# Memory values in two steps, pooling products in the logits' banks, and first values behind 24 key products

## The chip, the cores and the metric

The kernel runs on one core of a Trainium2 chip. Its time is device microseconds of one execution. The core has a matrix engine (TensorE, "PE" in the profile, with its weight loads as "PEld"), a vector engine (DVE), a scalar engine (ACT), a general engine (POOL) and a queue that issues transfers (SP). PE writes its products to PSUM, which the profile names by tile tags; DVE and ACT read them from there.

## What is computed

Two layers over 1024 tokens of width 1024. Both have gated cross-attention of four heads (128 wide) into 256 memory tokens. Layer 0 adds a gated causal pooling branch, layer 1 forgetting attention with 16 heads over keys and values that are projected once.

```python
def mixer_sublayer(x, mem, w_in, w_mem_kv, w_out, main_fn):
    h = x @ w_in                       # columns: main, mem q, main gate, mem gate
    ...
    y_main = main_fn(u_main)           # pooling, or forgetting attention
    y_mem = memory_attention(q_mem, mem, w_mem_kv)
    y = jnp.concatenate([y_main * jax.nn.silu(g_main), y_mem * jax.nn.silu(g_mem)], axis=-1)
    return y @ w_out

def causal_multiscale_pool(u, pool_w, pool_scale):
    ...                                # trailing mean of window 2/4/8/16 minus the token, by group
    mixed = jnp.einsum('bsgc,gcd->bsgd', pm, pool_w)
    return mixed.reshape(B, S, D_MAIN) * pool_scale

def memory_attention(q_mem, mem, w_mem_kv):
    ...
    p = jax.nn.softmax(logits, axis=-1)
    return jnp.einsum('bhsm,bmhd->bshd', p.astype(mv.dtype), mv).reshape(B, S, D_MEM)

def forgetting_attention(u, k, v, cum):
    # logit[t,s] = q_t.k_s/sqrt(Dh) + cum[t] - cum[s], causal, softmax, times v
```

`cum` is the running sum of the log forget gates. Then `x <- LayerNorm(alpha * x + y)` after each layer.

## The kernel before

**Products.** f32 operands are split in a high and a low part (`hi_lo`: a cast on ACT at L141, a subtraction on DVE at L142), and each product is made of three: high by high, high by low, low by high (`mm3`, L168). `slab` is the unit of projection: 128 output columns of a weight matrix by all 1024 tokens, 48 products of 512 columns (L184), in two halves of 512 tokens with 24 products each. A slab's accumulators are two PSUM banks of the tag "pj"; its weights come in two pieces of the tag "w", which has room for three pieces. Softmax weights and values are split in two f16 parts, and their products run in f16.

**PSUM.** Eight banks: "pj" 2, "L" 3 (logits), "T" 2, "O" 1. A tag's banks are used in turn, and a product that opens an accumulator waits until the bank's last user has been read.

**Orders.** PE's order is written out by hand in the memory attention of both layers and in all of the forgetting attention (`manual_schedule(engines={PE})`). Elsewhere, and for all other engines, a planner makes the order when the program is built. All queues then run in that order.

**Filling.** Inside the hand-written orders, `Fill` holds generators of slab products; `pump(cols)` issues products until so many columns of moving data are used up, and carries the remainder to the next call.

**Pooling** (`pool_group`, four times): two slabs `u`, running sums on DVE, two gate slabs, then four accumulators of six products each (L168 by way of `mm3`) in "pj". `gate` reads a gate slab from PSUM, a tanh on ACT (L197) and a product on DVE (L198); each pooling accumulator is then read on DVE (L530).

**Memory attention** (`mem_attention`, once a layer, behind pooling group 0 in layer 0 and first in layer 1). Ten steps. In steps 0 to 7 `probs(t)` makes the logits of 128 queries (12 products of 256 columns in "L"), the softmax on DVE and ACT (L297 to L308), and a transposing transfer (L312) to `pt[t]`. In steps 3, 5, 7 and 9 each of the four heads makes `values`: two accumulated sums of six f16 products for two tiles of queries, read on DVE with one multiplication (L324). Between all of these come products of the four memory gates' slabs. `pt` lies in the tag "T" of SBUF with six tiles.

**Start of the forgetting attention** (`start_units`): products of the first key slab, `v_first` (values of the first four heads and the forget gates' logits, 8 accumulators of 24 products, L606, whose weights lie in the four "MK" tiles that memory attention used for its keys and values), `forget_gates` (a chain of some 26 DVE instructions, L616 to L629, then a running sum on PE at L637 to L639 and a turned copy that goes to memory), `v_turned` with 24 products of the slab in between, the rest of the key slab and the query slab, and 48 products of the next pair's key slab. A key half is read by `k_evac` (L659 on ACT, L660 on DVE, twice each), a query half by `q_evac` (L670, L671).

Of the kernel before, what the change touches and what calls it, by code (L numbers as in the profile page):

```python
# [15 lines left out]
ALU = mybir.AluOpType  # L16
AX = mybir.AxisListType

P = 128
# [3 lines left out]
ST = S // P  # L23
NH = 512
HEADS = 16
MH = 4
# [9 lines left out]
LAG = 5  # L36
APART = 6 * NH
PSCALE = 2.0 ** 15
VALUES = {0: 52 * P, 4: 20 * P}


# [24 lines left out]
def run(units):  # L66
    for _ in units:
        pass
# [3 lines left out]
def trunk_kernel(ctx, tc, x, xT, memT, win, wk, wv0, wv, wmk, wmv, wout, poolw, pscale, lng, lnb, bforget, out):  # L72
# [5 lines left out]
    nc = tc.nc  # L78
# [22 lines left out]
    def ps(shape, tag, bufs):  # L101
        return psum.tile(shape, F32, tag=tag, name=nm(tag), bufs=bufs)
# [164 lines left out]
    def mem_attention(l, XH, XL, kv, qtile, ytile, yd):  # L267

        (kh, kl, v, undo), keys, vals = kv
        qs = []  # L270
        if l:
            for h in range(MH):
                keys(h)
        for h in range(MH):
            qh, ql = qtile(), qtile()
            run(slab(win[l, 8 + h], XH, XL, lambda cols, acc: hi_lo(qh[:, cols], ql[:, cols], acc)))
            qs.append((qh, ql))
            if not l:
                keys(h)
            vals(h)  # L280
        ys, gs = [ytile() for _ in range(MH)], [G() for _ in range(MH)]
        pt, fill = {}, Fill()
        for h in range(MH):
            fill.add(gate_units(win[l, 20 + h], gs[h], XH, XL), SLAB)

        def probs(i):

            p, two = sb([P, MH, NMEM], "P", 4), sb([P, 2, MH, NMEM], "P", 4, F16)
            m, ms, sm, r = tiny(MH), tiny(MH), tiny(MH), tiny(MH)
            for hp in range(2):  # L290
                lg = ps([P, 2, NMEM], "L", 3)
                for j in range(2):
                    h = 2 * hp + j
                    qh, ql = (t[:, i * P : (i + 1) * P] for t in qs[h])
                    mm3(lg[:, j, :], ((qh, kh[:, h, :]), (qh, kl[:, h, :]), (ql, kh[:, h, :])))
                pair = slice(2 * hp, 2 * hp + 2)
                nc.vector.tensor_reduce(m[:, pair], lg, AX.X, ALU.max, negate=True)  # L297
                nc.vector.tensor_scalar(ms[:, pair], m[:, pair], MSCALE, None, ALU.mult)
                for j in range(2):
                    h = 2 * hp + j  # L300
                    nc.scalar.activation(
                        p[:, h, :], lg[:, j, :], AF.Exp, bias=ms[:, h : h + 1], scale=MSCALE, accum_out=sm[:, h : h + 1],
                    )
            nc.vector.tensor_scalar(r, sm, 1.0 / PSCALE, None, ALU.mult)
            nc.vector.reciprocal(r, r)
            for h in range(MH):
                nc.scalar.activation(two[:, 0, h, :], p[:, h, :], AF.Copy, scale=r[:, h : h + 1])
                nc.vector.scalar_tensor_tensor(  # L308
                    two[:, 1, h, :], p[:, h, :], r[:, h : h + 1], two[:, 0, h, :], ALU.mult, ALU.subtract,
                )  # L310
            pt[i] = T([P, 2, MH, 2, P], F16)
            nc.sync.dma_start_transpose(  # L312
                pt[i].rearrange("p e h m q -> p (e h m) q"), two.rearrange("p e h t -> p (e h t)"),
            )

        def values(c, h):
            acc = ps([P, 2 * P], *(("O", 1) if h == 1 else ("T", 2)))
            for j in range(2):
                t = pt[2 * c + j]
                mm3(acc[:, j * P : (j + 1) * P], [  # L320
                    (v[:, h, 2 * e + m, :], t[:, f, h, m, :])
                    for m in range(2) for e, f in ((0, 0), (0, 1), (1, 0))
                ])
            nc.vector.tensor_scalar(ys[h][:, c * 2 * P : (c + 1) * 2 * P], acc, undo[:, h : h + 1], None, ALU.mult)  # L324

        with tc.manual_schedule(engines={PE}):
            for t in range(ST + 2):
                part = fill.left / (5 * (ST + 2 - t))
                if t < ST:
                    probs(t)  # L330
                fill.pump(part if t <= ST else 3 * part)
                for h in range(MH):
                    if t >= 3 and t % 2 == 1:
                        values((t - 3) // 2, h)
                    fill.pump(part if t <= ST else part / 2)
            fill.pump(float("inf"))
        for h in range(MH):
            nc.vector.tensor_tensor(ys[h], ys[h], gs[h], ALU.mult)  # L338
            nc.sync.dma_start(yd[:, h, :], ys[h])
# [143 lines left out]
    with tc.tile_pool(name="in0", bufs=1) as in0:  # L483

        def bt():
            return sb([P, S], "B", 8, F32R, in0)

        def pool_group(g):
            w = WINDOWS[g]
            pms = []  # L490
            for f in (2 * g, 2 * g + 1):
                u = sb([P, S], "P", 4)
                run(slab(
                    first[f] if g == 0 else win[0, f], XH, XL, lambda cols, acc: nc.scalar.copy(u[:, cols], acc),
                    ("L", 3) if f == 1 else ("pj", 2),
                ))
                cur, sh = u, 1
                while sh < w:
                    nxt = G()
                    nc.vector.tensor_tensor(nxt[:, sh:], cur[:, sh:], cur[:, : S - sh], ALU.add)  # L500
                    nc.vector.tensor_copy(nxt[:, :sh], cur[:, :sh])
                    cur, sh = nxt, 2 * sh
                pm = G()
                nc.vector.scalar_tensor_tensor(pm[:, w - 1 :], cur[:, w - 1 :], 1.0 / w, u[:, w - 1 :], ALU.mult, ALU.subtract)
                nc.vector.tensor_tensor(pm[:, : w - 1], cur[:, : w - 1], invc[:, : w - 1], ALU.mult)
                nc.vector.tensor_tensor(pm[:, : w - 1], pm[:, : w - 1], u[:, : w - 1], ALU.subtract)
                ph, pl = T(), T()
                hi_lo(ph, pl, pm)
                pms.append((ph, pl))
            r = raw([P, 2, 2 * P])  # L510
            nc.sync.dma_start(r, poolw[g])
            wh, wl = (MK([P, 2, 2 * P]) for _ in range(2))
            hi_lo(wh, wl, r)
            ys = []
            for f in (2 * g, 2 * g + 1):
                y = sb([P, S], "Y", 4, F32, in0)
                run(gate_units(win[0, 12 + f], y, XH, XL))
                ys.append(y)
            for d in range(2):
                f = 2 * g + d  # L520
                for n in range(2):
                    acc = ps([P, NH], "pj", 2)
                    terms = []
                    for ct in range(2):
                        a, b = wh[:, ct, d * P : (d + 1) * P], wl[:, ct, d * P : (d + 1) * P]
                        ph, pl = (t[:, n * NH : (n + 1) * NH] for t in pms[ct])
                        terms += [(a, ph), (a, pl), (b, ph)]
                    mm3(acc, terms)
                    yn = ys[d][:, n * NH : (n + 1) * NH]
                    nc.vector.scalar_tensor_tensor(yn, acc, pschalf[:, f : f + 1], yn, ALU.mult, ALU.mult)  # L530
                nc.sync.dma_start(y0d[f // 4, :, f % 4, :], ys[d])

        wtags = [("B", 8)] * 4 + [("W", 4)] * 2 + [("MK", 4)] * 2 + [("Y", 4)] * 2 + [("PG", 0), ("w", 0)]
        out_proj = OutProj(0, w_slots(wtags, in0), y0d)
        pool_group(0)
        kv = mem_kv(0)
        mem_attention(0, XH, XL, kv, bt, lambda: sb([P, S], "Y", 4, F32, in0), y0d[2])
        for g in range(1, 4):
            pool_group(g)
            out_proj.split((4, 12, 12)[g - 1])  # L540

        XH1, XL1 = (sb([P, KT, S], "A", 2, F32R) for _ in range(2))
        out_proj.rest(x, XH1, XL1, x1)
# [3 lines left out]
    with tc.tile_pool(name="in1", bufs=1) as in1:  # L547
# [137 lines left out]

        def start_units(own, following):

            yield from islice(own, 48)
            yield from v_first()
            gates = forget_gates()  # L690
            next(gates)
            for _ in v_turned():
                yield from islice(own, 6)
            yield from own
            yield from islice(following, 9)
            next(gates)
            yield from islice(following, 9)
            next(gates)
            yield from islice(following, 30)
# [61 lines left out]
        pt = {}  # L761
# [127 lines left out]
        with tc.manual_schedule(engines={PE}):  # L889
            own, following = pair_units(0), pair_units(1)  # L890
# [66 lines left out]
```

## Time and profile before

| what | value |
|---|---|
| runs of the kernel | 1254.17, 1254.45, 1252.7 us; median 1254.17 |
| the profiled execution | 1252.11 us, span 1250.3 us |
| granted TensorE clock, mean | 0.996 |
| ACT busy | 569.1 us (46%) |
| POOL busy | 171.1 us (14%) |
| DMA queue q1 | 54.4% of 16 engines |
| chain that ended last, share of PE | 94% |

A row of a timeline gives start and length in us, engine, line, operation, `out<-in`, shapes, a count where rows are merged, and in brackets the idle time ahead of it with what ended it. A row of a table by windows gives the stretch, its length, and for each engine the busy us with the number of instructions, then the granted clock, the DMA share and GB/s. Matmuls overlap: one of 512 columns is shown with 0.39 us or so, though the next starts much earlier.

### The profile page before, as it was taken

The numbers are of one execution on the slowest core, as the hardware profiler recorded it, in microseconds if no ns is written. First come the engines' busy times: TensorE is split into PE (matmuls) and PEld (weight loads), VectorE is DVE, ScalarE is ACT, GpSimd is POOL, SyncE is SP. The second block draws the span as 40 slices with busy tenths as digits, with TensorE's granted clock in tenths as the row PEclk, the third lists the DMA queues.
The fourth block names the chain that finished last, engine by engine and source line by source line (L and its number), as shares of the span: only waits on it lengthen the run. The fifth ranks groups of instructions, "written<-read, shape, count | busy, mean of one in ns | idle before, by whom it ended". The sixth has DMA issues, their size and how long they took to land.

```text
span 1250.3 us, 19605 instructions
## 1 busy us (share of the span) xinstructions
PE 1234.2 (99%) x7018; PEld 1038.3 (83%) x7018; DVE 793.7 (63%) x1869; ACT 569.1 (46%) x1241; POOL 171.1 (14%) x276
## 2 busy tenths in 40 slices
PE   9999999999999999999999999999999999999997
PEld 6888888888888888888897888888888888888885
DVE  6444766374644457357726888878877788775644
ACT  5233652242321123256424777767766677661110
POOL 0000000000000000000002343433334333430000
PEclk9999999999999999999999999999999999999998
DMA  6333544242363324234514778968887979884530
GB/s 227 100 103 87 124 110 138 90 118 86 101 219 118 118 93 135 71 106 108 173 52 129 167 171 183 185 165 177 180 185 153 196 186 213 228 242 160 175 106 34
DMA packets 267410, 178.64 MB, mean 143 GB/s; under 512 B 212273, under 2 KB 225713, under 8 KB 267313
## 3 DMA queue, kind: packets, MB, share of 16 engines
q1 hardware_dynamic: 267312, 177.40, 54.4%
q8 instruction: 55, 0.90, 0.3%
q14 instruction: 43, 0.34, 0.1%
HBM read 94.97 MB, written 22.61 MB: 94 GB/s over the span
## 4 chain that ended last, share of the span: by engine, by line
PE 94%; DVE 3%; DMA 1%; issue 0%; ACT 0%; POOL 0%; SPq 0%; DVEq 0%; POOLq 0%; ACTq 0%
PE pj L184 52%; PE L L388 9%; PE pj L388 9%; PE L L168 7%; PE O L168 6%; PE pj L217 3%; PE pj L606 2%; PE pj L168 1%; PE T L168 1%; PE T L388 1%; PE L L184 1%; PE O L388 1%; PE T L260 1%; DMA T<-P 1%; DVE w L142 0%
## 5 line engine op out<-in xcount | busy, mean ns | idle before, releaser
L184 PE MATMUL pj<-A,w 128*128 128x512 f32 x2928 | 709.4, 393 | 1.6 <-ACT A L141 1.6
L184 PEld LDWEIGHTS pj<-A,w 128*128 128x128 f32 x2928 | 540.3, 188 | 106.8 <-ACT A L141 2.5
L758 DVE SCALAR_TENSOR_TENSOR P<-T,s,P 128x512 f16<-128x512 f32 x192 | 111.7, 613 | 36.1 <-ACT P L757 35.1
L736 ACT ACTIVATE T<-MK,s 128x512 f32<-128x512 f32 x192 | 111.4, 580 | 46.6 <-DVE s L728 26.2
L142 DVE TENSOR_TENSOR w<-raw,w 128x512 fp32r<-128x512 f32 x106 | 73.8, 698 | 89.4 <-ACT w L141 88.9
L757 ACT ACTIVATE P<-T,s 128x512 f16<-128x512 f32 x192 | 102.9, 577 | 43.3 <-ACT T L736 18.2
L141 ACT CAST w<-raw 128x512 fp32r<-128x512 f32 x106 | 65.7, 621 | 114.5 <-PE pj L184 75.3
L168 PE MATMUL L<-B,B 128*128 128x512 f32 (+3 forms) x384 | 89.4, 341 | 0.7 <-DVE s L728 0.7
L633 POOL MEMSET G<- 128x128 f32 x1 | 0.2, 206 | 613.7 <-DVE V L338 613.7
L168 PEld LDWEIGHTS L<-B,B 128*128 128x128 f32 x384 | 70.6, 188 | 14.2 <-DVE s L728 1.1
L728 DVE CUSTOM_DVE_ANT_0 MK<-L,R 128x512 f32<-128x512 f32 (+3 forms) x128 | 72.7, 568 | 10.0 <-PE L L168 6.4
L168 PEld LDWEIGHTS <-V 128*128 128x128 f16 x1152 | 64.5, 98 | 9.2 <-issue 8.0
L142 DVE TENSOR_TENSOR T<-T,T 128x1024 fp32r<-128x1024 f32 x23 | 28.1, 1223 | 68.1 <-PE pj L388 49.9
L146 POOL TENSOR_TENSOR w<-raw,w 128x512 fp32r<-128x512 f32 x54 | 70.6, 1307 | 4.3 <-PE pj L184 0.5
L141 ACT CAST T<-T 128x1024 fp32r<-128x1024 f32 x23 | 24.2, 1052 | 101.9 <-DMA T<-y0d 52.1
L168 PE MATMUL O<-T,V 128*128 128x128 f16 x1152 | 69.9, 219 | 0.7 <-DMA T<-P 0.6
L720 POOL TENSOR_SCALAR_AFFINE_SELECT R<-R 128x128 f32<-128x128 f32 x128 | 42.1, 335 | 207.5 <-DVE s L728 161.5
L217 PE MATMUL pj<-T,w 128*128 128x256 f32 x384 | 48.9, 284 | 0.7 <-DVE s L444 0.4
L217 PEld LDWEIGHTS pj<-T,w 128*128 128x128 f32 x384 | 47.6, 191 | 2.0 <-DVE w L142 0.7
L388 PE MATMUL pj<-B,T 128*128 128x512 f32 x192 | 47.6, 389 | 0.0
L145 POOL TENSOR_SCALAR w<-raw 128x512 fp32r<-128x512 f32 x54 | 33.9, 628 | 89.8 <-PE pj L184 89.8
L388 PE MATMUL L<-B,T 128*128 128x512 f32 x168 | 43.3, 393 | 0.0
(208 smaller groups left out, 1584.4 us busy)
## 6 DMA issues: line engine op xcount, KB each, us to landing
raw<-in_win_dram SPq DMA_DIRECT2D x96, 256.0 KB, 2.8
raw<-in_wout_dram SPq DMA_DIRECT2D x40, 256.0 KB, 2.7
B<-B SPq DMA_DIRECT2D x32, 256.0 KB, 3.9
R<-cumd SPq DMA_DIRECT2D x16, 512.0 KB, 4.4
y0d<-Y SPq DMA_DIRECT2D x12, 512.0 KB, 2.6
T<-y0d SPq DMA_DIRECT2D x12, 512.0 KB, 3.9
T<-y1d SPq DMA_DIRECT2D x11, 512.0 KB, 4.1
raw<-in_wmk_dram SPq DMA_DIRECT2D x16, 256.0 KB, 2.6
```

Source lines behind the costliest of these rows:

```text
L141: pin(nc.scalar.copy(hi, src))
L142: pin(nc.vector.tensor_tensor(lo, src, hi.bitcast(F32), ALU.subtract))
L146: nc.gpsimd.tensor_tensor(lo, src, hi.bitcast(F32), ALU.subtract)
L168: nc.tensor.matmul(acc, a, b, start=i == 0, stop=i == len(terms) - 1)
L184: nc.tensor.matmul(accs[n], a[:, k, :], b[:, kt, n * NH : (n + 1) * NH], start=kt == 0 and i == 0, stop=kt == KT - 1 and i == 2,)
L217: nc.tensor.matmul(acc, w[:, k, :], m[pc][:, k, :], start=pc == 0 and k == 0 and i == 0, stop=pc == 1 and k == 3 and i == 2,)
L388: nc.tensor.matmul(accs[a][nh], y[:, k, a * P : (a + 1) * P], w, start=kt == 8 and i == 0, stop=kt == 7 and i == 2,)
L720: nc.gpsimd.affine_select(R[:, qs], R[:, qs], [[-1, P]], ALU.is_ge, -NEG, base=0, channel_multiplier=1).ins
L728: nc.vector.tensor_tensor_reduce(p[:, lo:up], lg, R[:, lo:up], 1.0, top, ALU.add, ALU.min, m[:, n : n + 1])
L736: nc.scalar.activation(e, p[:, lo:up], AF.Exp, bias=top, scale=-1.0, accum_out=sums[:, n, hd % 2, i : i + 1],)
L757: nc.scalar.activation(pair[:, lo:up], e, AF.Copy, scale=r)
L758: nc.vector.scalar_tensor_tensor(pair[:, L + lo : L + up], e, r, pair[:, lo:up], ALU.mult, ALU.subtract)
```

## The change

Three edits. **Memory values**: `values` takes four tiles of queries with a whole bank, in steps 5 and 9; the amount to fill is worked out so that each step has the same number of columns, counting those of the values (`MVALUES`), and is given out as 0.4 behind `probs` and 0.15 behind each head. **Pooling products** use the three "L" banks. **First values** of four heads come behind 24 products of the first key slab; the other 24 stand in `v_turned`, and the whole query slab behind it.

```diff
@@ -36,6 +36,7 @@
+MVALUES = MH * 4 * 6 * P
 VALUES = {0: 52 * P, 4: 20 * P}
@@ -314,25 +315,26 @@
         def values(c, h):
-            acc = ps([P, 2 * P], *(("O", 1) if h == 1 else ("T", 2)))
-            for j in range(2):
-                t = pt[2 * c + j]
+            acc = ps([P, NH], *(("O", 1) if h == 1 else ("T", 2)))
+            for j in range(4):
+                t = pt[4 * c + j]
                 mm3(acc[:, j * P : (j + 1) * P], [
                     (v[:, h, 2 * e + m, :], t[:, f, h, m, :])
                     for m in range(2) for e, f in ((0, 0), (0, 1), (1, 0))
                 ])
-            nc.vector.tensor_scalar(ys[h][:, c * 2 * P : (c + 1) * 2 * P], acc, undo[:, h : h + 1], None, ALU.mult)
+            nc.vector.tensor_scalar(ys[h][:, c * NH : (c + 1) * NH], acc, undo[:, h : h + 1], None, ALU.mult)
 
         with tc.manual_schedule(engines={PE}):
             for t in range(ST + 2):
-                part = fill.left / (5 * (ST + 2 - t))
+                todo = [MVALUES if k in (5, 9) else 0 for k in range(t, ST + 2)]
+                part = max(0, (fill.left + sum(todo)) / len(todo) - todo[0])
                 if t < ST:
                     probs(t)
-                fill.pump(part if t <= ST else 3 * part)
+                fill.pump(part * 0.4)
                 for h in range(MH):
-                    if t >= 3 and t % 2 == 1:
-                        values((t - 3) // 2, h)
-                    fill.pump(part if t <= ST else part / 2)
+                    if todo[0]:
+                        values((t - 5) // 4, h)
+                    fill.pump(part * 0.15)
             fill.pump(float("inf"))
@@ -519,7 +521,7 @@
                 for n in range(2):
-                    acc = ps([P, NH], "pj", 2)
+                    acc = ps([P, NH], "L", 3)
                     terms = []
@@ -685,7 +687,7 @@
         def start_units(own, following):
 
-            yield from islice(own, 48)
+            yield from islice(own, 24)
             yield from v_first()
```

## Prediction

> **What bounds the kernel now.** I read the header of the page first, then the list of who waited for whom on PE, then the timeline of PE alone round the three edited places.
>
> ```profile
> span 1250.3 us, 19605 instructions
> PE 1234.2 (99%) x7018; PEld 1038.3 (83%) x7018; DVE 793.7 (63%) x1869; ACT 569.1 (46%) x1241; POOL 171.1 (14%) x276
> ```
>
> ```profile
> engine line waited for: us in total, times, longest us
> ...
> PE pj L168 <- DVE Y L198: 1.4, 3, 0.5
> ...
> PE pj L606 <- DVE B L660: 0.4, 1, 0.4
> ...
> PE O L637 <- DVE G L629: 0.3, 1, 0.3
> ```
>
> PE is the bound from end to end: 1250.3 - 1234.2 leaves 16 us in which it isn't busy, and DVE, the next engine, has 37% to spare. The change adds and removes no product, so it can only win PE's gaps and the places where PE is busy but slower than its own pace. The three rows are the gaps that it touches. They understate the loss: a product's modelled end covers part of a gap, so I measure from start to start in the timeline.
>
> **Pooling products in the logits' banks.** Timeline of PE at the first pooling group, then a table by windows at all four:
>
> ```profile
> 52.10 1.52 PE L168 MATMUL pj<-T,MK 128*128 128x512 f32 x6
> 54.07 2.11 PE L168 MATMUL pj<-T,MK 128*128 128x512 f32 x8 [0.45 <-DVE Y L198]
> ```
>
> ```profile
> 52.10:53.23 1.13, 1.13 (x6) 0.94 (x5) 1.00 0.60 212
> 53.23:54.07 0.84, 0.39 (x3) 0.00 (x1) 1.00 0.00 0
> 54.07:57.60 3.53, 3.53 (x15) 2.92 (x16) 1.00 0.35 104
> 236.88:237.72 0.84, 0.39 (x3) 0.01 (x1) 1.00 0.00 0
> 286.62:287.47 0.85, 0.40 (x3) 0.01 (x1) 1.00 0.00 0
> 336.33:336.79 0.46, 0.40 (x3) 0.02 (x1) 1.00 0.00 0
> ```
>
> Five products start within 1.13 us, so the pace is 0.227 us. From the sixth to the seventh, which opens the second pooling accumulator, 0.84 us pass: 0.61 lost. The 15 steps behind it take 3.53 instead of 3.40: 0.13 more, in refilling the pipe. Groups 1 and 2 lose the same; in the last group another product filled the gap and only about 0.1 is lost. Sum: 3 x 0.74 + 0.1 = 2.3 us.
>
> The seventh product needs the "pj" bank in which the gate slab's second half stood, and its read on DVE (L198) ends late. In the "L" banks the first three accumulators find a bank that nobody has used for long; the fourth takes the first one's, 18 products (4.08 us) after the first began, 2.7 us after it ended. That one is read behind L198:
>
> ```profile
> 53.34 0.68 DVE L198 SCALAR_TENSOR_TENSOR Y<-Y,pj 128x512 f32<-128x512 f32 x1
> 53.93 0.74 DVE L530 SCALAR_TENSOR_TENSOR Y<-pj,pschalf,Y 128x512 f32<-128x512 f32 x1
> ```
>
> It is done at 54.67 and the fourth would start at 56.18: 1.5 us of room. Behind group 3 the output projection opens in an "L" bank; it takes the second accumulator's, two accumulators later, and its "pj" banks are now free. **-2.2 us**, between -2.3 and 0.
>
> **Memory values in two steps.** Rows of the timeline at the end of layer 0's memory attention, a later run of such products in the FoX heads, and the row of the FoX products by tile:
>
> ```profile
> 179.54 7.98 PE L184 MATMUL pj<-A,w 128*128 128x512 f32 x34
> 187.36 0.84 PE L168 MATMUL T<-T,MK 128*128 128x128 f16 x12
> 188.01 0.72 PE L184 MATMUL pj<-A,w 128*128 128x512 f32 x2
> 188.57 0.84 PE L168 MATMUL O<-T,MK 128*128 128x128 f16 x12
> 189.22 0.71 PE L184 MATMUL pj<-A,w 128*128 128x512 f32 x2
> ```
>
> ```profile
> 775.77 3.08 PE L168 MATMUL O<-T,V 128*128 128x128 f16 x52
> ```
>
> ```profile
> L168 PE MATMUL O<-T,V x1152: 217/219/230, 701.9 to 1120.3; 128*128 128x128 f16 x192
> ```
>
> 52 products take 3.08 us with the last one's own 0.219, so the steps are 0.056. A block of 12 from 187.36 to 188.01 is 0.65, near 12 x 0.056 = 0.67. But the two gate products behind it take 0.56 (188.01 to 188.57) where two cost 0.45. So each round trip between f32 and f16 products costs 0.10 - 0.02 = 0.08 us, with no wait shown. Before, each layer makes 16 such trips (4 steps x 4 heads, gate products between). After, `part` is 0 in steps 5 and 9, so the four heads of a step run as one block of 96, and two trips per layer stay: 2 x 14 x 0.08 = 2.2 us. **-2.2 us**, with 0.07 to 0.09 a trip -2.0 to -2.5.
>
> TensorE: Matmul & The Clock Gate of the Trainium skill (section Part 2, step 1) says that the queue pulls weight loads ahead of products in flight; by that a trip is free and this term 0. The rows differ by 0.08 us a trip, and I go by them.
>
> What the two blocks can wait for. Each step now has 12 logit products and 24 gate products or 96 value products, 1.4 + 5.4 = 6.9 us (steps 8 and 9: 5.4). Tile 7 is the tight one: its logits come in step 7, its transposed halves are needed in step 9.
>
> ```profile
> 171.75 1.59 PE L168 MATMUL L<-MK,B 128*128 128x256 f32 x12
> ```
>
> ```profile
> 179.47 1.58 SPq L312 DMA_TRANSPOSE T<-P  x1
> ```
>
> ```profile
> DMA to landing us min/median/max: 3.6/3.7/5.4
> ```
>
> From logits to issue 7.7 us, to landing 11.4 (13.1 with the longest landing). Step 9 begins 6.9 + 5.4 = 12.3 us after these logits, and the first product on tile 7 is the 19th of its block, 1.0 us on: 13.3. Room 1.9 us, 0.2 with the longest landing. Before it was 187.36 - 171.75 = 15.6. I take no stall, and keep 1 to 2 us a layer as a rival. The fourth head's block needs the first head's bank back 2.7 us after its last product; its read on DVE, half again as long as this:
>
> ```profile
> L324 DVE TENSOR_SCALAR V<-T,undo 128x256 f32<-128x256 f32 x2 | 1.0, 478 | 0.0
> ```
>
> takes some 0.75 us (L530 above reads 512 columns in 0.74), so there are 2 us for DVE to be elsewhere. Tile 6's transpose reuses tile 0's buffer, free when step 5 ends, a step before tile 6's halves exist.
>
> **First four heads' values behind 24 products.** Timelines of PE and DVE in layer 1, then two pieces of the chain that ended last:
>
> ```profile
> 614.51 11.63 PE L184 MATMUL pj<-A,w 128*128 128x512 f32 x50
> 625.98 3.19 PE L606 MATMUL pj<-MK,A 128*128 128x272 f32 x24
> 629.55 2.63 PE L606 MATMUL pj<-MK,A 128*128 128x272 f32 x19 [0.38 <-DVE B L660]
> ```
>
> ```profile
> 656.66 9.14 PE L184 MATMUL pj<-A,w 128*128 128x512 f32 x39
> 666.15 0.46 PE L637 MATMUL O<-G,G 128*128 128x128 f32 x2 [0.35 <-DVE G L629]
> ```
>
> ```profile
> 618.82 1.14 DVE L142 TENSOR_TENSOR MK<-raw,MK 128x272 fp32r<-128x272 f32 x3
> 621.36 0.68 DVE L660 TENSOR_TENSOR B<-pj,B 64x512 fp32r<-64x512 f32 x1 [1.40 <-ACT B L659]
> 622.07 0.69 DVE L142 TENSOR_TENSOR w<-raw,w 128x512 fp32r<-128x512 f32 x1
> 622.79 0.69 DVE L660 TENSOR_TENSOR B<-pj,B 64x512 fp32r<-64x512 f32 x1
> ```
>
> ```profile
> 651.41 0.19 DVE G L609
> ...
> 664.65 1.36 DVE G L629
> ```
>
> The forget gates take DVE from 651.41 to 666.01, 14.6 us, under 63 products and 16 transposes; PE arrives 39 x 0.228 = 8.9 us after 656.66, at 665.6, and waits 0.5, with 0.1 to refill. 24 of the 48 key products now stand behind the values, so the cover grows by 24 x 0.227 = 5.4 us. The evacuation of the second key half falls into the chain now (two L660, 1.4 us), that of the first query half falls out. The stall goes: **-0.6 us**. Next late is the copy of the sums, nine products on; those nine are unchanged.
>
> What gets less cover are the values' weights: 5.4 instead of 10.9 us. Their last parts (L142, MK) are ready at 619.96, 5.4 us after the last block of values ended (614.51), since they need its buffer; the fifth k-tile is used 24 x 0.227 + 12 x 0.127 = 7.0 us after it (24 of them show 3.19 with a tail of 0.29, so 0.127 each). 1.5 us of room. DVE's queue there gets longer reads but loses a gate's L198. The second value accumulator still waits for the key half evacuated just before (629.55 instead of 625.98 + 24 x 0.127 = 629.0, 0.5 lost and 0.1 to refill): the first half's evacuation ended at 623.48, 2.9 us after its last product, where 3.05 are covered. So this stall is between 0 and 0.9; I take 0.5: **-0.1 us**. SP issues the same loads; the query slab's second weight piece must now await the first key piece's release in the transposes' stretch, 24 products ahead of its use, 5.4 us for a cast and a subtraction of 0.69 each: nothing.
>
> **Sum.** 2.2 + 2.2 + 0.6 + 0.1 = 5.1 us. The profiled execution took 1252.1 us (span 1250.3 and 1.8 round it), which gives 1247.0; it lies 2.1 below the median of the runs, 1254.2. On the median: **1249.0 us**.
>
> **Rivals.**
> 1. The blocks of values wait. For: room falls from some 4.5 us to 1.9, and no gate product is left in steps 5 and 9 to fill a hole. Against: no later tile's chain stands beside tile 7's on DVE and ACT. At 1.3 us a layer: 1251.6.
> 2. The bank change yields nothing: the planner, which orders DVE itself, puts other work ahead of the first pooling read and the fourth accumulator waits as long as the second did. For: that is how L198 came late. Against: 1.5 us of room. 1249.0 + 2.2 = 1251.2.
> 3. Slower: long blocks of f16 products run at the pace of their weight loads, 0.098 us instead of 0.056, since no 512-column product stands beside them.
>
> ```profile
> L168 PEld LDWEIGHTS <-V 128*128 128x128 f16 x1152 | 64.5, 98 | 9.2 <-issue 8.0
> ```
>
> 384 products x 0.042 = 16.1: 1265.1. It decides from (5.1 + 2.5) / 384 = 0.020 us a product. Against: the 52 products in a row above kept 0.056. The same page of the Trainium skill (Back-to-back issue gap) gives 81 ns for sustained 128-column pairs; 25 ns more than the trace would be an estimated 9.6 us, 1258.6, but the row of 52 disagrees; its chance is within this rival's.
>
> **How the numbers follow.** Forecast 0.66 (1247.5 to 1250.5), first rival 0.18, second 0.10, third 0.03, others on the slow side 0.03. A measurement tells 0.2%, 2.5 us, from no change, so faster means below 1251.7. The forecast, most of the second and half of the first fall there: 0.80. Slower takes the third and the others, 0.06; 0.14 remain within 0.2%. The range reaches 1 us under the forecast's own, for the switch and bank terms at their high ends, and up through both milder rivals: 1246.5 to 1253.0.
>
> **What would show it.** Right: no row of PE L168 waiting on L198; four blocks of 96 f16 products without gate products between, 5.4 us each; PE L637 no longer waiting on L629. Wrong: PE waiting on a transposed tile or on L324 at step 9, L168 waiting on L530 in the "L" banks, L606 waiting on L142 or for over 0.9 us on L660.

## The result, and the profile after

| | before | changed |
|---|---|---|
| median of 6 runs of each | 1253.33 us (1251.88 to 1254.45) | 1246.24 us (1245.73 to 1248.17) |
| ratio | | 0.9946, interval 0.9933 to 0.9959 |
| profiled execution | 1252.11 us, span 1250.3 | 1246.03 us, span 1244.3 |

The changed kernel is faster by 6.8 us (1253.33 x 0.0054; by the interval 5.1 to 8.4). A second series gave 0.9957 (0.9944 to 0.9969), 5.4 us. The forecast was 5.1 us less, or 1249.0 us.

The changed kernel has one line more near the top and a second one more behind `values`, so L168 is now L169, L198 is L199, L530 is L532, L637 is L639, L728 is L730. The list of who waited for whom on PE, changed kernel (us in total, times, longest):

```profile
PE L L169 <- DVE s L730: 1.6, 1, 1.6
...
PE O L169 <- ACT T L738: 0.9, 1, 0.9
PE pj L185 <- ACT A L142: 0.9, 2, 0.6
PE pj L218 <- ACT w L142: 0.4, 1, 0.4
PE pj L608 <- DVE B L662: 0.3, 1, 0.3
```

Two rows of before are gone: the pooling products' wait on the gate's read (L198) and the running sum's wait on the forget gates (L629). The row of the first values (now L608) is still there, as the prediction kept it. On top stands a wait that was 0.7 us before: that of the first logits of the FoX heads (the heads of the forgetting attention).

**Pooling.** Timelines of PE and then of DVE at group 0 of the changed kernel:

```profile
50.56 5.60 PE L169 MATMUL L<-T,MK 128*128 128x512 f32 x24
56.00 0.39 PE L185 MATMUL pj<-A,w 128*128 128x512 f32 x1
```

```profile
51.80 0.68 DVE L199 SCALAR_TENSOR_TENSOR Y<-Y,pj 128x512 f32<-128x512 f32 x1
52.40 0.74 DVE L532 SCALAR_TENSOR_TENSOR Y<-L,pschalf,Y 128x512 f32<-128x512 f32 x1
53.48 0.75 DVE L532 SCALAR_TENSOR_TENSOR Y<-L,pschalf,Y 128x512 f32<-128x512 f32 x1 [0.34 <-PE L L169]
```

All 24 products now stand in one row: 5.44 us to the next slab, 24 x 0.227. The gate's read (L199) is as late as it was, 1.24 us behind the first pooling product, but nobody waits for it. The first pooling read ends at 53.14, 1.5 us before the fourth accumulator starts (50.56 + 18 x 0.227 = 54.65), the room that was forecast.

**Memory values.** Timeline of PE at the end of layer 0's memory attention, changed kernel:

```profile
180.72 2.65 PE L185 MATMUL pj<-A,w 128*128 128x512 f32 x11
183.21 1.51 PE L169 MATMUL T<-T,MK 128*128 128x128 f16 x24
184.56 1.50 PE L169 MATMUL O<-T,MK 128*128 128x128 f16 x24
185.90 2.84 PE L169 MATMUL T<-T,MK 128*128 128x128 f16 x48
188.56 1.63 PE L185 MATMUL pj<-A,w 128*128 128x512 f32 x6
```

The block of 96 takes 188.56 - 183.21 = 5.35 us, 0.0557 a product, without a gap between the heads. Tables by windows, first before, then the changed kernel, each from the first memory logits to the start of the next stage, with 480 products begun in each (layer 0, then layer 1):

```profile
124.89:192.17 67.28, 67.28 (x482) 56.44 (x481) 47.47 (x121) 37.89 (x114) 0.00 (x0) 1.00 0.47 121
...
547.77:615.05 67.28, 67.28 (x482) 56.45 (x481) 47.90 (x124) 41.76 (x121) 0.03 (x1) 1.00 0.47 116
```

```profile
122.61:188.56 65.95, 65.95 (x483) 58.09 (x481) 46.04 (x113) 39.06 (x115) 0.00 (x0) 1.00 0.48 123
542.53:608.54 66.01, 66.01 (x483) 58.12 (x481) 44.94 (x115) 41.79 (x122) 0.00 (x0) 1.00 0.49 112
```

1.33 and 1.27 us less. PE is busy for the whole of each window before and after (first two numbers of a row): this gain is not to be found in any list of waits, only in the length of the stage.

**First FoX logits.** Timelines of PE there, changed kernel:

```profile
659.45 0.38 PE L639 MATMUL O<-G,G 128*128 128x128 f32 x2
...
673.67 0.61 PE L169 MATMUL L<-B,B 128*128 128x512 f32 x2
675.87 0.62 PE L169 MATMUL L<-B,B 128*128 128x384 f32 x2 [1.59 <-DVE s L730]
```

The sum at 659.45 waits for nothing any more. The fourth logits' bank waits 1.59 us for the first read on DVE (L730), which needs the rows R from memory.

### The profile page after: what moved, and what is told of

It reads as the page before. It is cut to its first block, busy times and chain, and to the rows that moved or that the text cites. A ratio compares the mean times of both kernels' runs of the same rounds, so it can differ in the third digit from the quotient of the medians.

```text
span 1244.3 us, 19599 instructions
## 1 busy us (share of the span) xinstructions
PE 1229.6 (99%) x7018; PEld 1041.0 (84%) x7018; DVE 789.3 (63%) x1853; ACT 568.6 (46%) x1241; POOL 171.5 (14%) x276
## 5 line engine op out<-in xcount | busy, mean ns | idle before, releaser
L185 PE MATMUL pj<-A,w 128*128 128x512 f32 x2928 | 701.3, 392 | 0.9 <-ACT A L142 0.9
L142 ACT CAST w<-raw 128x512 fp32r<-128x512 f32 x106 | 65.7, 621 | 106.2 <-PE pj L185 68.8
L169 PE MATMUL L<-B,B 128*128 128x512 f32 (+3 forms) x384 | 89.4, 341 | 1.6 <-DVE s L730 1.6
L169 PEld LDWEIGHTS L<-B,B 128*128 128x128 f32 x384 | 70.6, 188 | 15.0 <-DVE s L730 2.0
L730 DVE CUSTOM_DVE_ANT_0 MK<-L,R 128x512 f32<-128x512 f32 (+3 forms) x128 | 72.6, 567 | 11.5 <-PE L L169 6.7
L169 PEld LDWEIGHTS <-V 128*128 128x128 f16 x1152 | 64.4, 98 | 9.3 <-issue 9.3
L142 ACT CAST T<-T 128x1024 fp32r<-128x1024 f32 x23 | 24.2, 1052 | 103.3 <-DMA T<-y0d 52.7
L169 PE MATMUL O<-T,V 128*128 128x128 f16 x1152 | 69.9, 219 | 0.9 <-ACT T L738 0.9
```

The source lines that it names most:

```text
L142: pin(nc.scalar.copy(hi, src))
L169: nc.tensor.matmul(acc, a, b, start=i == 0, stop=i == len(terms) - 1)
L185: nc.tensor.matmul(accs[n], a[:, k, :], b[:, kt, n * NH : (n + 1) * NH], start=kt == 0 and i == 0, stop=kt == KT - 1 and i == 2,)
L730: nc.vector.tensor_tensor_reduce(p[:, lo:up], lg, R[:, lo:up], 1.0, top, ALU.add, ALU.min, m[:, n : n + 1])
```

## The experiments

Two theories stood against each other. **One:** the three edits add up, each in its own stage, to 5 to 5.5 us, and what the profiled pair shows beyond that belongs to the single executions. **Two:** one of the edits does more than its own stage shows, or the gain of the values is the order of other work, not the round trips.

The stage lengths below are read from the timelines of PE, from the start of one stage's first product to the start of the next one's. "Again" is a second profile of the kernel to its left.

| stage, us | before | changed | again | banks only | values only | start only | banks + values | sum earlier | again |
|---|---|---|---|---|---|---|---|---|---|
| to the first memory logits | 124.90 | 122.61 | 123.95 | 122.66 | 123.32 | 123.00 | 123.56 | 122.46 | 122.65 |
| memory attention, layer 0 | 67.29 | 65.95 | 65.95 | 67.29 | 65.95 | 67.29 | 65.95 | 65.95 | 65.95 |
| pooling 1 to 3, output, norm | 355.59 | 353.97 | 353.97 | 353.90 | 355.64 | 355.58 | 353.99 | 353.99 | 354.02 |
| memory attention, layer 1 | 67.29 | 66.01 | 65.95 | 67.29 | 65.95 | 67.29 | 65.95 | 66.00 | 65.95 |
| key slab to the first FoX logits | 61.98 | 61.73 | 61.29 | 61.96 | 62.31 | 61.30 | 62.34 | 61.21 | 61.30 |
| first FoX heads, to the 200th value product | 87.58 | 88.44 | 87.78 | 91.06 | 90.75 | 90.86 | 91.44 | 86.49 | 86.49 |
| from there to the last product | 476.43 | 476.40 | 476.39 | 476.40 | 476.42 | 476.41 | 476.41 | 476.41 | 476.48 |

### Each edit alone

```diff
 a_banks: the kernel before with
-                    acc = ps([P, NH], "pj", 2)
+                    acc = ps([P, NH], "L", 3)
 b_values: the kernel before with the edits of values() and of the loop of steps
 c_start: the kernel before with
-            yield from islice(own, 48)
+            yield from islice(own, 24)
 ab_nostart: the first two together
```

> The kernel before with the pooling products in the three L banks and nothing else. Theory 1 (the three edits add up, each in its own place): the three gaps of 0.84 us in the pooling groups close, 2.3 us less in those stages, ratio 0.998. Rival (the gap only moves to the fourth pooling accumulator or the next stage): ratio 1.000, with a wait of L168 on L530 in place of the one on L198.

> The kernel before with the memory values by 512 queries in two steps and nothing else. Theory 1: both memory attention stages get 1.1 to 1.25 us shorter, 2.4 us in all, ratio 0.998. Rival (the values hold more than that, for instance through what DVE and SP do behind them): 3.5 us or more, ratio 0.997.

> The kernel before with the first values behind 24 key products and nothing else. Theory 1: the wait of 0.5 us ahead of the running sum of the forget gates goes, ratio 0.9995. Rival 1 (the wait for the first rows R at the start of the FoX heads grows because of this edit, as in the changed kernel, by 0.8 us): no gain, ratio 1.000 to 1.0005, and a gap of some 1.7 us at the fourth logits' bank. Rival 2 (the 1 to 1.5 us that the change won beyond the forecast stand here): ratio 0.998.

> The changed kernel with the first values behind 48 key products again. Theory 1: 0.2 to 0.7 us slower than the changed kernel, ratio to before 0.9955 to 0.996. Rival 1: 0.3 us faster than the changed kernel, ratio 0.994. Rival 2: 2 us slower, ratio 0.9965.

Measured, as ratios to before: banks 0.9975 (0.9963 to 0.9987), values 0.998 (0.9967 to 0.9993), start 0.9989 (0.9977 to 1.0), banks and values 0.9965 (0.9951 to 0.998). The single edits multiply to 0.9944, the changed kernel's own ratio is 0.9946. The intervals reach 1.4 to 1.9 us either way, too wide to separate the rivals of the values and of the start: banks and values together, by theory 1 at 0.9955 to 0.996, came out at 0.9965, the figure of rival 2, with 0.996 inside the interval. The stages separate them. An edit shortens its own stage to the same length alone as with the others, 355.59 to 353.90 for the banks, 67.29 to 65.95 for the values, 61.98 to 61.30 for the start. For the values the expectation had 1.1 to 1.25 a layer; it was 1.3. One edit also acts outside its stage: with the values and the old start (`b_values`, `ab_nostart`) the stage behind them is 0.35 us longer, 62.31 and 62.34, and the wait of the first values on the key half is 0.7 us there instead of 0.4.

Rival 2 of the start edit falls by its stage: alone it is worth 0.7 us there, not 2. Rival 1 expected some 1.7 us at the fourth logits' bank because of this edit. The gap is there in `c_start` with 2.4 us, but it is as large where the start is untouched: 2.3 in `b_values`, 2.7 in `a_banks`, 3.1 in `ab_nostart`. The same place in `a_banks`, then in the changed kernel's second profile:

```profile
679.81 1.01 PE L168 MATMUL L<-B,B 128*128 128x384 f32 x2 [2.69 <-DVE s L728]
```

```profile
676.07 0.62 PE L169 MATMUL L<-B,B 128*128 128x384 f32 x2 [0.93 <-DVE s L730]
```

So this gap is not made by the start edit. Over the nine kernels and executions that have it, it is 0.7 to 3.1 us, and the profile of before happened to have the shortest.

The gap costs more than its own length. A table by windows of `a_banks` behind it (the third number from the end is the granted clock):

```profile
679.75:683.16 3.41, 3.35 (x8) 2.79 (x9) 2.38 (x9) 1.88 (x5) 0.59 (x2) 0.50 0.89 193
```

For 3.41 us PE had half its clock. The stage is 91.06 - 87.58 = 3.5 us longer than before; the longer gap makes up 2.0 of it (2.69 - 0.72), and the slower clock the rest. The profiles of `b_values`, `c_start`, `ab_nostart` and `t_banks` (below) have the same stretch of 3.41 us, beginning between 0.1 us ahead of the gap's end and 1.4 us behind it. In these five the stage of the first FoX heads is 90.8 to 91.5 us; in the four profiles with a shorter gap and the full clock (before, the two of the changed kernel and `trips32` below) it is 87.6 to 89.1.

### The changed kernel again

> The changed kernel once more, profiled again. Theory 1: the 1.5 us that its first slabs were shorter than before's, and the 0.9 us that its first FoX logits waited longer, are of that one execution: both differ by some tenths to 1 us here. Rival: they are of the kernel, and stand here again within 0.2 us.

Ratio 0.9957 (0.9944 to 0.9969). The part before the first memory logits is 1.3 us longer than in the first profile, though the program is the same, and the gap at the FoX logits 0.7 us shorter; all stages between agree to 0.1, but for the one of the key slab with 0.4. The rival falls: the two places differ between executions of one program by as much as the start edit is worth, or more, and the expectation's 1 us was exceeded once. In the first of them the rows at the very start show it: PE waited 1.29 us for its first split operand (L142 on ACT) in the second profile and 0.65 in the first, and the next products stepped at 0.43 us (8.43 to 8.86) where the first profile has 0.23 (6.97 to 7.20). Theory 1 holds so far as the stages between are concerned.

### Two banks that nobody has just left

```diff
 the kernel before with
-                    acc = ps([P, NH], "pj", 2)
+                    acc = ps([P, NH], "T", 2)
```

> The kernel before with the pooling products in the two T banks. If what counted is that the second accumulator finds a bank that no gate slab has just left, two are enough: the gaps of 0.84 us close as with the three L banks (third accumulator starts 2.7 us behind the first, which is read by 2.6). If the third bank is needed, a wait on L530 of 0.1 to 0.5 us a group is left.

One execution was profiled. Timeline of PE at group 0:

```profile
51.59 5.65 PE L168 MATMUL T<-T,MK 128*128 128x512 f32 x24
```

There is no gap; the stage of pooling groups 1 to 3 is 353.95 us, as with the three "L" banks. The whole execution took 1253.18 us, which says nothing about a term of 2 us: it is a single one, and its gap at the FoX logits was 3.1 us. The number of banks isn't what counted. The second accumulator must not stand in the bank that the gate slab has just left.

### Sixteen round trips a step

```diff
 the changed kernel with
-MVALUES = MH * 4 * 6 * P
+MVALUES = 2048
@@ values
                     for m in range(2) for e, f in ((0, 0), (0, 1), (1, 0))
                 ])
+                fill.pump(NH)
@@ the loop of steps
-                fill.pump(part * 0.4)
+                fill.pump(0 if todo[0] else part * 0.4)
...
-                    fill.pump(part * 0.15)
+                    fill.pump(0 if todo[0] else part * 0.15)
```

> The changed kernel with one gate product behind every six value products in steps 5 and 9: 16 round trips a step instead of one, 30 more a layer, the same products in all. Theory 1 (a round trip between f32 and f16 products costs 0.08 us): 60 x 0.08 = 4.8 us slower than the changed kernel, ratio to before 0.998 to 0.999. Rival (the gain of the values was not the trips but the order of other work around them): within 1 us of the changed kernel, ratio 0.995.

Ratio to before 1.0003 (0.9994 to 1.0012), median 1252.67 us, 5.4 us over the changed kernel in the same series. The stages of memory attention are 68.77 and 68.40 us, 2.8 and 2.45 more than in the changed kernel's second profile for 30 more trips each; 0.4 of the 2.8 is a wait for tile 7's transfer in layer 0. Timelines of PE in step 5, then of its weight loads (PEld):

```profile
154.97 0.48 PE L185 MATMUL pj<-A,w 128*128 128x512 f32 x1
155.30 0.51 PE L169 MATMUL T<-T,MK 128*128 128x128 f16 x6
155.61 0.48 PE L185 MATMUL pj<-A,w 128*128 128x512 f32 x1
```

```profile
154.95 0.19 PEld L185 LDWEIGHTS pj<-A,w 128*128 128x128 f32 x1
155.29 0.34 PEld L169 LDWEIGHTS <-MK 128*128 128x128 f16 x6 [0.15 <-issue]
```

One round is 155.61 - 154.97 = 0.64 us, where 0.227 + 6 x 0.056 = 0.563 would do: 0.08 a trip, without a wait in the row. The rival falls: the same products, with the values in the same two steps, lose the whole gain when the trips come back. (The gate products are spread otherwise over the steps, 16 of them now in steps 5 and 9.) The rule of the Trainium skill that weight loads are pulled ahead of products in flight (TensorE: Matmul & The Clock Gate, Part 2, step 1) would, as the prediction reads it, make a trip free; the measurement decides against that.

The rows show where the 0.08 stands. The f32 product behind an f16 block is recorded with 0.48 us instead of 0.39, and the next start comes 0.33 behind it instead of 0.227, while the six f16 products take 0.31 instead of 0.334. Its weight load takes 0.19 us, an f16 one 0.10, and the f16 product ahead of it has only 0.056 us to cover it. That the longer load isn't covered would explain the cost, but no run tried it.

### The running sum nine products earlier

If the start edit gives the forget gates more cover than they need, the sum can come earlier, and with it the rows R.

```diff
 the changed kernel with
             yield from own
-            yield from islice(following, 9)
             next(gates)
             yield from islice(following, 9)
             next(gates)
-            yield from islice(following, 30)
+            yield from islice(following, 39)
```

> The changed kernel with the running sum of the forget gates nine products earlier: right behind the query slab, the nine products stand behind its turned copy. If the cover that the start edit added is to spare (the gates' chain ends at 653.1 us, PE comes to the sum at 659.5), nothing waits at the sum, the rows R land 2.0 us earlier against the FoX heads, and the gap of 1.75 us at the fourth logits' bank closes: 1.5 to 1.8 us faster than the changed kernel, ratio to before 0.993. If R's landing moves with the B transfers behind it, half of that: 0.994.

> The kernel with the sum nine products earlier once more, beside the changed kernel's two runs: ratio to before 0.993 to 0.994, and again no wait of the FoX heads' first logits on the rows R, if that wait is closed and not merely short by chance.

Ratio 0.9936 (0.9924 to 0.9948) and 0.9932 (0.9918 to 0.9946), medians 1244.35 and 1243.82 us; the changed kernel in the first of these series had 1247.24, and its fastest execution there, 1245.75, is above the slowest of this version, 1245.51. This version beats both kernels, by more than expected: 2.9 us under the changed kernel instead of 1.5 to 1.8. Timeline of PE:

```profile
656.73 0.38 PE L639 MATMUL O<-G,G 128*128 128x128 f32 x2
...
660.64 9.12 PE L185 MATMUL pj<-A,w 128*128 128x512 f32 x39
...
672.99 0.96 PE L169 MATMUL L<-B,B 128*128 128x512 f32 x4
```

Nothing waits at the sum, and the fourth logits' bank follows the third at once. The gap is closed, not short by chance: the stage of the first FoX heads is 86.49 us in both profiles, against 87.6 to 91.5 in the others of the table. That is 1.3 and 1.95 us under the changed kernel's two profiles. The rest may lie in the clock, which is not shown: two of the changed kernel's five executions in that series had a mean granted clock of 0.996, and none of this version's eleven was below 0.997. Queue of SP, changed kernel and then this one:

```profile
664.03 3.59 SPq L649 DMA_DIRECT2D cumd<-G  x8
669.62 0.36 SPq L151 DMA_DIRECT2D raw<-in_win_dram  x1
670.21 0.34 SPq L707 DMA_DIRECT2D R<-cumd  x1
671.07 3.21 SPq L665 DMA_DIRECT2D B<-B  x4
```

```profile
661.31 3.58 SPq L649 DMA_DIRECT2D cumd<-G  x8
666.08 0.81 SPq L706 DMA_DIRECT2D R<-cumd  x2
668.93 0.34 SPq L151 DMA_DIRECT2D raw<-in_win_dram  x1
```

R is issued 3.5 us ahead of the first FoX logits (669.59 - 666.08) instead of 0.06 (670.27 - 670.21). Two of these are the nine products. The rest is the queue: in the changed kernel R stood behind a load of weights that was issued only at 669.62; here it stands ahead of that load.

### The same with 48 key products ahead

```diff
 the kernel with the earlier sum, with
-            yield from islice(own, 24)
+            yield from islice(own, 48)
```

> The kernel with the sum nine products earlier, but with the first values behind 48 key products as before. If the cover that the start edit gives is what makes the earlier place free: PE waits 2.5 us at the running sum (0.5 as before and nine products of 0.227 less ahead of it), while the gap at the FoX heads' first logits still closes: about 2 us slower than early9, ratio to before 0.995 to 0.996. Rival (the gates' chain is done early anyway): as early9, 0.9935.

Ratio 0.9983 (0.9973 to 0.9993), median 1250.11: 6.3 us slower than with 24, not 2. Timeline of PE:

```profile
660.87 0.46 PE L639 MATMUL O<-G,G 128*128 128x128 f32 x2 [2.35 <-DVE G L631]
661.16 1.63 PE L641 MATMUL O<-G,G 128*128 128x112 f32 x14
662.65 3.82 PE L185 MATMUL pj<-A,w 128*128 128x512 f32 x9
```

The wait at the sum is 2.35 us, where 2.5 were expected. Behind it the nine products take 666.26 - 662.65 = 3.6 us, and the same nine in the kernel with 24 key products 2.2. Tables by windows of the two stretches, 48 and then 24 key products:

```profile
662.65:666.26 3.61, 3.61 (x11) 2.69 (x11) 0.98 (x2) 0.59 (x1) 0.00 (x0) 0.56 0.62 156
```

```profile
658.43:660.61 2.18, 2.18 (x11) 1.73 (x11) 0.98 (x2) 0.44 (x1) 0.30 (x1) 1.00 1.07 233
```

The granted clock is 0.56 instead of 1.00: the stretch of 3.41 us at half clock stands here behind the wait at the sum, and takes 1.4 us more that the expectation did not have. The first values lose another 1.0 on the key half. From the key slab to the FoX logits it is 66.2 us, 5.0 more than with 24 key products; the gap at the FoX logits is closed, as expected. So the start edit, worth 0.7 us alone, is what makes the earlier sum possible.

## Why the prediction was right

- **Bound.** PE stayed at 99%. Of the stages that no edit touches, the long one behind the first FoX heads is as long as before to 0.1 us. The part up to the first memory logits and the first FoX heads are not: they differ by 1 to 2 us for the reasons above, and the prediction did not reckon with that.
- **Banks, -2.2.** Measured in groups 1 to 3: 1.6 to 1.7 us; in group 0, 24 products take 5.44 us where they took 0.74 more: 2.4 in all. The room of 1.5 us for the fourth accumulator was there. The second rival (the wait moves to L530) did not come.
- **Values, -2.2.** Measured 1.33 and 1.27, 2.6 us. The step was right: round trips with no wait to be seen. The size was a little low: the prediction let two trips a layer stay, but the last one's cost falls on the first products of the next stage, so 15 leave this one, at 1.33 / 15 = 0.089 us. What the values cost behind them, the 0.35 us at the first values, the prediction did not have; in the changed kernel the start edit takes it away.
- **Tile 7.** The first rival did not come, but the room was smaller than written, and in layer 1 there was next to none. In layer 0 the issue came 8.4 us after the logits, not 7.7.

```profile
170.87 1.59 PE L169 MATMUL L<-MK,B 128*128 128x256 f32 x12
```

```profile
179.28 1.32 SPq L313 DMA_TRANSPOSE T<-P  x1
```

  With 3.7 to landing that is 183.0; the block began at 183.21, and its first product on this tile a microsecond later. In layer 1 of the same profile:

```profile
599.01 3.01 SPq L313 DMA_TRANSPOSE T<-P  x1
```

```profile
DMA to landing us min/median/max: 5.1/5.1/5.1
```

```profile
603.13 1.51 PE L169 MATMUL T<-T,MK 128*128 128x128 f16 x24
```

  The tile landed at 604.1 and its first product started 18 x 0.056 = 1.0 us into the block, at 604.1 too. In layer 1 of `early9` and `early9_k48` landing took 5.3 and 5.4 us, and that product came 0.06 and 0.18 us late. That nothing was lost here was luck.
- **Start, -0.7.** Right in size alone (0.68 in its stage). In the changed kernel it shows as 0.25 and 0.69 in the two profiles, and as 0.6 and 1.05 against banks and values without it (62.34), since it also takes away what the values cost there. The prediction counts 63 products under the gates' chain; its timeline has 57 (6 + 6 + 6 + 39). Its sum goes by the last 39 and is not touched by that. The wait at the sum went; the wait of the first values stayed, at 0.3 in one profile and none in the list of the other, within the 0 to 0.9 that was given.
- **Slower rival.** Blocks of 96 run at 0.056 us a product, so long blocks don't fall back to the pace of their weight loads (0.098 us). The 81 ns that the Trainium skill gives for sustained 128-column pairs (TensorE: Matmul & The Clock Gate, Back-to-back issue gap) do not hold for these f16 blocks.
- **The total.** The terms measured by stage are 2.4 + 2.6 + 0.3 to 0.7 = 5.3 to 5.7 us. The two ratios give 6.8 and 5.4, with intervals that hold this sum. The median, 1246.24, lies 2.8 under the forecast of 1249.0, and 0.3 under the lower end of the range, 1246.5. The forecast stood on three runs of before with a median of 1254.17; on that base the ratio of 0.9946 gives 1247.4. The runs beside which 1246.24 was measured have 1253.33, so the base makes up 0.8 of the 2.8; larger series of before gave 1252.03, 1252.01 and 1251.69. The other 2.0 is the difference of the medians, 7.1 instead of 5.1. The stages of the edits hold 0.2 to 0.6 of it; the rest is not shown to belong to the change, and in the second series the medians differ by 4.8.

## What to carry to other kernels

Where an engine is busy all the time, compare the length of a stage with its products times their pace: a cost per switch between two kinds of work (0.08 us here, 5 us when 60 of them were added) stands in no list of waits. When a bank is waited for, first ask whether another tag's banks lie idle at that time; it need not be more of them. And a wait on memory at the head of a stage differed by 0.7 us between two executions of one program and by 2.4 us between kernels that issue it at the same place, so compare the stages that an edit touches before the totals, and look at the granted clock behind a wait.

## What was not expected of the hardware

The rows R land at different times though they are issued at the same place (0.06 us ahead of the first FoX logits in every kernel but the ones with the earlier sum): from issue to landing it was 3.9 us in the profile of before, 4.8 and 4.1 in two of the changed kernel, and 5.5 to 6.3 in the others, and the gap that follows was 0.7, 1.6 and 0.9, and 2.3 to 3.1. Transfers between the B tiles are issued 0.86 us behind R and run beside it; whether they set the landing was not tried. With the earlier sum they are issued 4.3 us behind R, and R lands after 4.0 us, no sooner than in the profile of before.

A wait of PE of 2.3 us or more was followed by 3.41 us at half clock in six profiles: the five with the long gap at the FoX logits and the one that waits 2.35 us at the sum. `trips32`, with a gap of 2.29, kept its full clock there. What decides this was not tried.

The part up to the first memory logits also differs, 122.6 and 123.95 us in two profiles of the same program. In the profile of before, with 124.9, the granted clock is 0.50 from 7.85 to 11.26 us, behind a wait of 1.4 us; that is up to 1.7 us of this profile's length.
